# An 8-row tile moved from last to first, and a last 12-row tile summed on two engines and stored in halves

## The chip, the core and the metric

The kernel runs on one core of one Trainium2 chip. The metric is the device time of one execution in microseconds (us); lower is better. Engines that matter: DVE (VectorE), ACT (ScalarE), and the sixteen DMA engines, which move data between the chip's main memory (HBM) and the core's working memory (SBUF, 128 partitions). SP (SyncE) only issues DMAs here.

## What is computed

Each row of 1,024 numbers is divided by the sum of its absolute values.

```python
x = np.random.randn(32, 512, 1024).astype(np.float32)
sums = np.sum(np.abs(x), axis=-1, keepdims=True)
out = (x / (sums + 1e-8)).astype(np.float32)
```

There are 32 x 512 = 16,384 rows of 4 KB: 67.11 MB are read and as many written.

## The kernel before, in words

The 16,384 rows are dealt to 128 partitions, 128 rows each. They are worked through in tiles; `rows` (L31 to L33) is the list of how many rows per partition each tile has: ten tiles of R = 12 and one of the remaining 8, at the end. `piece` (L35) gives tile i's part of the input or output: partition p holds k consecutive rows, so what a DMA moves per partition is one contiguous run (48 KB for 12 rows, 32 KB for 8).

One loop (L70) runs over the tiles, in the order as written. For each tile:

- L72: SP issues one DMA that loads the tile into `x_tile`. The pool `sbuf` has BUFS = 4 buffers, so from the fifth tile on SP waits until the store from four tiles before has landed.
- L45: DVE sums the absolute values of all k rows in one instruction, into `s`. L52 adds EPS and L54 takes the reciprocal, both on k numbers per partition.
- L55: DVE multiplies the first kv = k - k // 3 rows by their reciprocals, in place (8 of 12, 6 of 8). L62: ACT multiplies the other rows, one instruction of 1,024 elements per partition for each (4 of 12, 2 of 8).
- L74: ACT issues one DMA that stores the tile. The issue waits for DVE's multiply and ACT's last row.

Loads thus go through SP's DMA queue (q1 in the profile) and stores through ACT's (q10). Within an engine the order is that of the program; between the engines semaphores order what depends on each other.

Of the kernel before, what the change touches and what calls it, by code (L numbers as in the profile page):

```python
# [1 line left out]

# [4 lines left out]

FP32 = mybir.dt.float32
EPS = 1e-8


@with_exitstack
def kernel(
    ctx: ExitStack,
    tc: tile.TileContext,
    x: bass.AP,
    out: bass.AP,
):
    nc = tc.nc
    P = nc.NUM_PARTITIONS  # L20

    x_flat = x.flatten_outer_dims()
    out_flat = out.flatten_outer_dims()
    n, d = x_flat.shape


    R = 12
    BUFS = 4
    per_partition = n // P
    assert n % P == 0  # L30
    rows = [R] * (per_partition // R)  # L31
    if per_partition % R:
        rows.append(per_partition % R)  # L33

    def piece(flat, i):  # L35
        a, k = P * sum(rows[:i]), rows[i]
        return flat[a : a + P * k, :].rearrange("(p r) d -> p r d", p=P)

    sbuf = ctx.enter_context(tc.tile_pool(name="sbuf", bufs=BUFS))
    stats = ctx.enter_context(tc.tile_pool(name="stats", bufs=4))  # L40

    def normalize(x_tile, r0, k, kv):

        s = stats.tile([P, R], FP32)
        nc.vector.tensor_reduce(  # L45
            out=s[:, :k],
            in_=x_tile[:, r0 : r0 + k, :],
            axis=mybir.AxisListType.X,
            op=mybir.AluOpType.add,
            apply_absolute_value=True,  # L50
        )
        nc.vector.tensor_scalar_add(out=s[:, :k], in0=s[:, :k], scalar1=EPS)  # L52
        inv = stats.tile([P, R], FP32)
        nc.vector.reciprocal(out=inv[:, :k], in_=s[:, :k])  # L54
        nc.vector.tensor_mul(  # L55
            out=x_tile[:, r0 : r0 + kv, :],
            in0=x_tile[:, r0 : r0 + kv, :],
            in1=inv[:, :kv].unsqueeze(2).to_broadcast([P, kv, d]),
        )
        for r in range(kv, k):  # L60
            row = x_tile[:, r0 + r, :]
            nc.scalar.activation(  # L62
                out=row,
                in_=row,
                func=mybir.ActivationFunctionType.Copy,
                scale=inv[:, r : r + 1],
            )

    with tc.manual_schedule():
        for i, k in enumerate(rows):  # L70
            x_tile = sbuf.tile([P, R, d], FP32)
            nc.sync.dma_start(out=x_tile[:, :k, :], in_=piece(x_flat, i))  # L72
            normalize(x_tile, 0, k, k - k // 3)
            nc.scalar.dma_start(out=piece(out_flat, i), in_=x_tile[:, :k, :])  # L74


# [1 line left out]
_INS = ['x']  # L78
_OUTS = [((32, 512, 1024), 'float32')]


# [23 lines left out]
```

## Time and profile before

| | |
|---|---|
| Time, median of 9 executions | 317.2 us (317.08 to 317.56) |
| Time of the profiled execution | 317.41 us |
| Its span in the profile | 315.8 us |
| DVE busy | 235.8 us (75%) |
| ACT busy | 46.1 us (15%) |
| Moved by DMA | 134.23 MB, 425 GB/s over the span |
| Load of a 12-row tile, issue to landing, median | 34.6 us |
| Store of a 12-row tile, issue to landing, median | 51.9 us |

The span runs from the first to the last event that the profiler recorded; the execution's time is 1.6 us longer. In rows of the profile, L45 is line 45 of the kernel, `out<-in` names the buffers, and "idle before" is the time that the engine stood idle just before the instruction, with what ended it. SPq and ACTq are the sequencers of SP and ACT, which issue DMAs; a DMA's own transfer shows in the share of the DMA engines, in the queues' shares, and in the waits of others.

### The profile page before, as it was taken

Reading aid. Unit: us, or ns where it says so; the run is one execution under the profiler, and the core shown is the slowest. Engines: PE = TensorE matmul, PEld = TensorE weight load, DVE = VectorE, ACT = ScalarE, POOL = GpSimd, SP = SyncE. Lnnn points to the kernel's source line nnn. Section 1 sums busy time; section 2 is a strip of 40 time slices with the busy share of each in tenths; the row PEclk is TensorE's granted clock in tenths of the full one; section 3 lists DMA queues with packets and bytes.
Section 4 is the critical chain, followed back from the end, with each engine's and each line's share of the span. In section 5 each row is a group of like instructions: output and inputs, shape, how many; then the busy total and the mean of one; then the engine's idle time right before and its main releaser. Section 6 shows DMA issues by size and latency. Waiting matters only on the chain.

```text
span 315.8 us, 205 instructions
## 1 busy us (share of the span) xinstructions
DVE 235.8 (75%) x44; ACT 46.1 (15%) x43; POOL 0.2 (0%) x4
## 2 busy tenths in 40 slices
DVE  0069999999999599739946991998399569979400
ACT  0010501303105003200500050022005000502000
POOL 0000000000000000000000000000000000000000
DMA  8999999999999999999999999999999999999996
GB/s 324 448 423 423 461 361 442 405 461 436 398 473 423 417 467 411 423 461 411 423 455 417 442 442 411 448 442 411 430 443 417 442 432 446 413 442 448 405 425 299
DMA packets 3169, 134.23 MB, mean 425 GB/s; under 512 B 352, under 2 KB 352, under 8 KB 352
## 3 DMA queue, kind: packets, MB, share of 16 engines
q1 hardware_dynamic: 1584, 67.11, 49.9%
q10 hardware_dynamic: 1584, 67.11, 49.1%
q14 instruction: 1, 0.01, 0.0%
HBM read 67.11 MB, written 67.11 MB: 425 GB/s over the span
## 4 chain that ended last, share of the span: by engine, by line
another core or an unknown queue 36%; DMA 30%; DVE 26%; SPq 0%; issue 0%; DVEq 0%; ACTq 0%
DMA out_dram<-x_tile 15%; DVE s L45 15%; DMA x_tile<-in_x_dram 15%; DVE x_tile L55 10%; SPq L72 0%; DVE inv L54 0%; DVE s L52 0%; DVEq L54 0%; ACTq L74 0%
## 5 line engine op out<-in xcount | busy, mean ns | idle before, releaser
L45 DVE TENSOR_REDUCE s<-x_tile 128x12 f32<-128x12288 f32 (+1 forms) x11 | 138.2, 12563 | 58.0 <-DMA x_tile<-in_x_dram 58.0
L55 DVE TENSOR_TENSOR x_tile<-x_tile,inv 128x8192 f32<-128x8192 f32 (+1 forms) x11 | 93.5, 8498 | 0.4
L62 ACT ACTIVATE x_tile<-x_tile,inv 128x1024 f32<-128x1024 f32 x42 | 44.9, 1136 | 226.5 <-DVE inv L54 226.5
L62 ACT ACT_TABLE_LOAD x1 | 1.3, 1283 | 18.4 <-DMA x_tile<-in_x_dram 18.4
L54 DVE RECIPROCAL inv<-s 128x12 f32<-128x12 f32 (+1 forms) x11 | 2.5, 226 | 0.9
L52 DVE TENSOR_SCALAR s<-s 128x12 f32<-128x12 f32 (+1 forms) x11 | 1.9, 173 | 0.4
L89 POOL MEMSET const-uint8-127<- 128x1 uint8 x1 | 0.1, 102 | 0.0
L89 POOL MEMSET const-bfloat16-1.0<- 128x1 bf16 x1 | 0.1, 101 | 0.0
L89 POOL MEMSET const-float32-0.0<- 128x1 f32 x1 | 0.1, 98 | 0.2 <-issue 0.2
L89 POOL MEMSET const-float32-1.0<- 128x1 f32 x1 | 0.1, 98 | 0.0
## 6 DMA issues: line engine op xcount, KB each, us to landing
x_tile<-in_x_dram SPq DMA_DIRECT2D x10, 6144.0 KB, 34.6
out_dram<-x_tile ACTq DMA_DIRECT2D x10, 6144.0 KB, 51.9
x_tile<-in_x_dram SPq DMA_DIRECT2D x1, 4096.0 KB, 29.5
out_dram<-x_tile ACTq DMA_DIRECT2D x1, 4096.0 KB, 19.2
```

What stands on the lines that cost most here:

```text
L45: nc.vector.tensor_reduce(out=s[:, :k], in_=x_tile[:, r0 : r0 + k, :], axis=mybir.AxisListType.X, op=mybir.AluOpType.add, apply_absolute_v ...
L52: nc.vector.tensor_scalar_add(out=s[:, :k], in0=s[:, :k], scalar1=EPS)
L54: nc.vector.reciprocal(out=inv[:, :k], in_=s[:, :k])
L55: nc.vector.tensor_mul(out=x_tile[:, r0 : r0 + kv, :], in0=x_tile[:, r0 : r0 + kv, :], in1=inv[:, :kv].unsqueeze(2).to_broadcast([P, kv, d]),)
L62: nc.scalar.activation(out=row, in_=row, func=mybir.ActivationFunctionType.Copy, scale=inv[:, r : r + 1],)
L89: nc = _bacc.Bacc("TRN2", target_bir_lowering=False, num_devices=1)
```

## The change

Two things are done together.

The list `rows` gets its 8-row entry in front: the tiles are 8, then ten times 12. The loads of the first four tiles, which wait for no buffer, so cover 44 rows where they covered 48, and the last tile has 12 rows.

The last tile is worked through in two halves of 6 rows, each with a sum, a reciprocal, a multiply and a store of its own. In each half DVE sums 3 rows, and ACT sums the other 3 with one activation (Abs with an accumulator) per row, whose elementwise result goes to a scratch tile `junk` in PSUM, the other on-chip memory. Each of the two engines also multiplies 3 rows. The tile's load stays one DMA. All other tiles are worked as before (`ks` = k; 6 and 2 rows, or 8 and 4, in the multiply).

```diff
     if per_partition % R:
-        rows.append(per_partition % R)
+        rows.insert(0, per_partition % R)
...
+    psum = ctx.enter_context(
+        tc.tile_pool(name="psum", bufs=1, space=bass.MemoryType.PSUM)
+    )
+    junk = psum.tile([P, d], FP32)
+
-    def normalize(x_tile, r0, k, kv):
+    def normalize(x_tile, r0, k, ks, kv):
...
         nc.vector.tensor_reduce(
-            out=s[:, :k],
-            in_=x_tile[:, r0 : r0 + k, :],
+            out=s[:, :ks],
+            in_=x_tile[:, r0 : r0 + ks, :],
...
+        for r in range(ks, k):
+            nc.scalar.activation(
+                out=junk[:, :],
+                in_=x_tile[:, r0 + r, :],
+                func=mybir.ActivationFunctionType.Abs,
+                accum_out=s[:, r : r + 1],
+            )
...
-            normalize(x_tile, 0, k, k - k // 3)
-            nc.scalar.dma_start(out=piece(out_flat, i), in_=x_tile[:, :k, :])
+            final = i == len(rows) - 1
+            h = k // 2 if final else k
+            for r0 in range(0, k, h):
+                if final:
+                    normalize(x_tile, r0, h, h // 2, h // 2)
+                else:
+                    normalize(x_tile, r0, h, h, h - h // 3)
+                nc.scalar.dma_start(
+                    out=piece(out_flat, i)[:, r0 : r0 + h, :],
+                    in_=x_tile[:, r0 : r0 + h, :],
+                )
```

In the built program the order on DVE is, for each half, the sum of 3 rows, the add, the reciprocal and the multiply. On ACT it is three sums, three multiplies and the store's issue for the first half, and then the same for the second; each sum after the first waits for the one before it.

## The prediction

> **What bounds the kernel now.** I read the page first: the share of the DMA queues, before any engine.
>
> ```profile
> span 315.8 us, 205 instructions
> ...
> DVE 235.8 (75%) x44; ACT 46.1 (15%) x43; POOL 0.2 (0%) x4
> ...
> DMA  8999999999999999999999999999999999999996
> ...
> q1 hardware_dynamic: 1584, 67.11, 49.9%
> q10 hardware_dynamic: 1584, 67.11, 49.1%
> ```
>
> The two queues, q1 for loads (issued by SP) and q10 for stores (issued by ACT), fill 49.9 + 49.1 = 99.0% of the sixteen DMA engines' time: 312.6 us of 315.8. No order of the work can win more than the 3.2 us left, unless the packets themselves become shorter. Next, where those 3.2 us lie: busy time by stretches (columns: stretch, its length, DVE, ACT, POOL busy, clock, DMA share, GB/s).
>
> ```profile
> 0.00:2.00 2.00, 0.00 (x0) 0.00 (x0) 0.20 (x4) 1.00 1.01 295
> 2.00:250.00 248.00, 198.14 (x36) 39.68 (x37) 0.00 (x0) 1.00 1.00 429
> 250.00:279.65 29.65, 22.05 (x4) 4.26 (x4) 0.00 (x0) 1.00 1.00 433
> 279.65:295.54 15.89, 15.62 (x4) 2.19 (x2) 0.00 (x0) 1.00 1.01 439
> 295.54:313.40 17.86, 0.00 (x0) 0.00 (x0) 0.00 (x0) 1.00 0.96 416
> 313.40:315.80 2.40, 0.00 (x0) 0.00 (x0) 0.00 (x0) 1.00 0.00 0
> ```
>
> The share is 1.00 from 2 us to the last store's issue at 295.54. A packet is counted where it starts, so the last two rows say: packets go out until the end of the drain, and then the last ones finish. By the trace's packet records the first starts at 1.72 us and the last ends at 314.35; a packet of 49,152 B (one partition of a 12-row tile) takes 1.815 us in the median, one of 32,768 B 1.213 us. Each engine carries 8 packets of each tile: 20 x 8 x 1.815 + 2 x 8 x 1.213 = 309.8 us. The rest up to 312.5 us is slow packets: 0.8 us per engine at the first load, 1.15 us around 42 us, shortly after the first store is issued (40.62), some 0.5 us between 148 and 231.
>
> Third, the end, in order of time, where a summary of the chain would name the vector engine:
>
> ```profile
> 277.79 0.34 ACTq L74 DMA_DIRECT2D out_dram<-x_tile  x1
> 279.65 8.69 DVE L45 TENSOR_REDUCE s<-x_tile 128x8 f32<-128x8192 f32 x1 [1.96 <-DMA x_tile<-in_x_dram]
> 288.38 0.17 DVE L52 TENSOR_SCALAR s<-s 128x8 f32<-128x8 f32 x1
> 288.65 0.20 DVE L54 RECIPROCAL inv<-s 128x8 f32<-128x8 f32 x1
> 288.89 6.56 DVE L55 TENSOR_TENSOR x_tile<-x_tile,inv 128x6144 f32<-128x6144 f32 x1
> 288.89 2.19 ACT L62 ACTIVATE x_tile<-x_tile,inv 128x1024 f32<-128x1024 f32 x2 [15.62 <-DVE inv L54]
> 295.54 0.34 ACTq L74 DMA_DIRECT2D out_dram<-x_tile  x1
> ```
>
> The last tile takes 15.89 us from landing to the store's issue, and it looks like the tail. It isn't: at 439 GB/s the engines are meanwhile draining earlier stores, and the packet records put the last packet of the store before it at 304.67, 9.1 us after the last store is queued.
>
> **What the Trainium skill says.** "DMA: Bandwidth & Descriptors", section "Queues, rings and completion order": each DMA engine takes turns between the queues that have work, packet by packet. The trace agrees: a 12-row load alone takes 8 x 1.815 = 14.5 us, beside stores 29.0 us (tiles land at 226.46 and 255.48). Its section "Where 436 GB/s comes from" puts the ceiling at 435 GB/s and says that HBM traffic is held to about 358; the trace has 429 to 439, so the ceiling holds here and the lower figure doesn't. "ScalarE: Activation LUTs", section "What ACT_TABLE_LOAD costs", prices an activation at 186 ns + 0.833 ns per element, and 93 ns for a per-partition operand: 1.132 us for L62, as traced (1.132 in the median); its section "Table sets: the hidden batching unit" says that abs is in every set, so Abs beside Copy needs no second table load.
>
> **The change part by part.**
>
> Durations, from the groups by form (busy, mean ns):
>
> ```profile
> L45 DVE TENSOR_REDUCE s<-x_tile 128x12 f32<-128x12288 f32 x10 | 129.5, 12951 | 56.1 <-DMA x_tile<-in_x_dram 56.1
> L55 DVE TENSOR_TENSOR x_tile<-x_tile,inv 128x8192 f32<-128x8192 f32 x10 | 86.9, 8692 | 0.3
> ```
>
> With the 8-row forms above, a row costs (12.95 - 8.69) / 4 = 1.066 us in the sum, with 0.16 fixed, and the same in the multiply ((8.69 - 6.56) / 2).
>
> *Packets.* The bytes stay. The last tile's store becomes two, so each engine gets 16 packets of 24,576 B for 8 of 49,152. From the two sizes a packet costs 11 ns + 0.0367 ns per byte, so 8 x 11 = 0.09 us more, and one more completion packet of 9 ns: +0.1 us. Lower bound 0; upper bound 0.3 us, if the fixed part were thrice as large on shorter packets.
>
> *The 8-row tile first.* It lands 14.5 - 9.7 = 4.8 us sooner, at 18.39 - 4.8 = 13.6, and is stored after 15.9 us, at 29.5 instead of 40.62. This starts stores 11 us earlier and gains nothing, since until then the loads fill the engines. Four loads are still in flight, 44 rows for 48. First packet of store 0: 4.4 us after its issue, as before (45.04 against 40.62), so 33.9. Then 8 turns of 1.213 + 1.815: done at 58.1, landed at 60.3 (2.2 us after the last packet, as for the loads: 253.29 and 255.48). SP's wait for it (the fifth load's) is covered: of the 24 load packets after tile 0, 11 are through at 33.9 and 8 more at 58.1; 5 are left, 18 us in turns. Store 1 is issued at 29.5 + 22.1 = 51.6, before store 0 ends.
>
> *The end.* Now both queues take turns, 8 x 3.63 = 29.04 us per 12-row tile. Store k ends at 58.1 + 29.04k, load 3 at 58.1 + 5 x 3.63 = 76.3, load 10 at 76.3 + 7 x 29.04 = 279.6; it lands at 281.8. Tile 9 lands at 252.7 and its store is queued at 274.9. Store 7 ends at 261.4; store 8 takes 5 turns beside loads until 279.6, then 3 packets alone: 285.0. Store 9: 285.0 + 14.5 = 299.5. So the engines have other work until 299.5, and half 1 has to be queued by then, less a lead of up to 4.4 us as at the first store.
>
> *The halves.* Half 1: DVE sums 3 rows in 3 x 1.066 + 0.16 = 3.4 us, beside it ACT sums 3. The trace has no Abs with an accumulator. Lower bound: the skill's 1.04 us each, 3.1 us. Upper bound: 1.13 us plus 0.4 for the accumulator and the wait on ACT's own semaphore that the build puts between them, 4.6. I take 3.6. The add and the reciprocal with gaps: 0.6. Multiply: DVE 3 rows, 3.4, beside three ACT rows at 1.07 each. Issue 0.1: 7.7 us in all (7.5 to 8.7), at 289.5. Half 2: DVE goes straight on; ACT's three sums are queued behind the store's issue, which waits for DVE's multiply: 0.4 more, 8.1 us, so 297.6 (to 299.5). Half 1's packets keep the engines until 299.5 + 7.3 = 306.8. Both are queued 9 to 10 us ahead (7 at the upper bounds), so summing on both engines and the split cost and bring nothing in time; DVE was idle before this tile lands (274.9 to 281.8), so nothing waits behind them.
>
> What if that cover were absent? A plain 12-row tile takes 22.1 us from landing to store: 281.8 + 22.3 = 304.1, that is 4.6 us after the engines run out, plus a lead of up to 4.4. So moving the 8-row tile alone costs 4.6 to 9 us, and the halves take exactly that back. Sum against the profiled execution (317.41 us, span 315.8): +0.1, 317.5. It lies 0.2 over the median of 317.2, so against the median: 317.3.
>
> **The rivals.** *Faster: the slow packets go.* The 1.15 us at the first store could fall away or be shared with the cold first loads, as the store now comes earlier; or the engines' ends, spread over 313.17 to 314.35, draw together with half-sized packets. For it: nothing else in the span is loose. Against it: the loads in flight at the first store are as many as before. 317.3 - 1.15 = 316.1.
>
> *Slower: the store queue starts cold twice.* Store 1 is queued 6.5 us before store 0 ends; with the lead of 4.4 us only 2.1 us are left. If store 0 is quicker by over 2.1 us, the queue runs dry near 56 us and may stall the loads by 1.15 us again: 318.4. Against it: the engines go on loading, and the stall may belong to the very first use.
>
> *Slower: the tail is bare.* If ACT's sums are far dearer, half 1 misses 299.5. It decides from 17.7 us (less the lead, 13.3) between landing and store. At the plain tile's 22.3 us: 317.3 + 4.6 = 321.9 or more. Against it: it needs sums of over 3 us a row where the price is 1.1.
>
> **How the numbers follow.** Forecast (no change; its own range 316.8 to 317.9): 0.78. Slow packets gone: 0.10. Cold start twice: 0.07. Bare tail: 0.05. About 0.2% (0.63 us) is what a measurement of this kernel can tell from no change, so faster 0.10, same 0.78, slower 0.12. The range goes from 316.4, most of the way to the faster case, to 318.4, the cold start; the bare tail and the rest of the faster case stay outside.
>
> **What would show it.** The two queues again at 99% of the engines; the last load landing near 282; two stores issued near 290 and 298 while the DMA share stays at 1.00 until about 313; one table load; the first store issued near 29.5. I'm wrong if the DMA share drops before the drain (near 56 us or after 299), or if the slow load packets at the first store are missing or come twice.

## The result, and the profile after

The changed kernel takes 319.52 us (median of 9 executions, 319.19 to 320.07) against 317.24 (29 executions): a ratio of 1.007, 95% interval 1.0062 to 1.0079. That is 2.3 us slower, outside the predicted range of 316.4 to 318.4. Its profiled execution took 319.41 us, with a span of 317.6. Three more executions took 319.91, 317.49 and 322.76 us; they are not among the nine, and the last counts as a slow run.

The page of the changed kernel, the lines that answer to those of before:

```profile
span 317.6 us, 226 instructions
...
DVE 228.0 (72%) x48; ACT 55.2 (17%) x57; POOL 0.2 (0%) x4
...
DMA  8999999999999999999999999999999999999994
...
q1 hardware_dynamic: 1584, 67.11, 49.5%
q10 hardware_dynamic: 1728, 67.11, 48.8%
```

The queues' share fell from 99.0% to 98.3%, but of a longer span: 0.983 x 317.6 = 312.2 us, as good as the 312.6 before. So the packets cost what they did. What was added is time in which DMA engines do nothing, and the stretches say where (columns as in the prediction):

```profile
2.00:284.10 282.10, 213.94 (x40) 41.87 (x39) 0.00 (x0) 1.00 1.00 430
284.10:299.35 15.25, 14.06 (x8) 13.34 (x18) 0.00 (x0) 1.00 0.97 418
299.35:312.00 12.65, 0.00 (x0) 0.00 (x0) 0.00 (x0) 1.00 1.00 431
312.00:313.00 1.00, 0.00 (x0) 0.00 (x0) 0.00 (x0) 1.00 0.97 418
313.00:314.00 1.00, 0.00 (x0) 0.00 (x0) 0.00 (x0) 1.00 0.23 98
314.00:315.00 1.00, 0.00 (x0) 0.00 (x0) 0.00 (x0) 1.00 0.17 74
315.00:316.00 1.00, 0.00 (x0) 0.00 (x0) 0.00 (x0) 1.00 0.06 25
```

There is no hole in the middle and none before the drain. The end is ragged instead. One packet of 24,576 B started in a stretch of 1 us shows as 25 GB/s: from 315 to 316 us, one of sixteen engines starts one packet, and the other fifteen have none left to start. The kernel before, in the same stretches, starts no data packet after 314 us:

```profile
312.00:313.00 1.00, 0.00 (x0) 0.00 (x0) 0.00 (x0) 1.00 0.91 393
313.00:314.00 1.00, 0.00 (x0) 0.00 (x0) 0.00 (x0) 1.00 0.23 98
314.00:315.00 1.00, 0.00 (x0) 0.00 (x0) 0.00 (x0) 1.00 0.00 0
```

The packet records show the same engine by engine. (Packets carry no engine number; I followed each engine from one packet's end to the next one's start. The completion packets of the last store, 4 B each and one per engine, give the same ends without that.)

| us | before | after |
|---|---|---|
| Mean of the sixteen engines' last packets | 313.82 | 313.84 |
| First engine done | 313.17 | 313.03 |
| Last engine done | 314.35 | 316.43 |
| Time of the profiled execution less the last engine's end | 3.06 | 2.98 |

The mean moved by 0.02 us; the last engine moved by 2.08, and the time with it. A slow packet is one that takes longer than the median of its size (1.815 us for 49,152 B); what counts below is the excess. After 60 us, three engines of the changed kernel collect 1.42, 1.60 and 2.43 us of it, while nine have 0.1 us or less. Before, each engine had between 0.3 and 0.9.

The end on the compute engines is as planned:

```profile
284.12 3.35 DVE L52 TENSOR_REDUCE s<-x_tile 128x3 f32<-128x3072 f32 x1 [6.98 <-DMA x_tile<-in_x_dram]
285.08 0.19 ACT L60 ACTIVATION_READ_ACCUMULATOR junk<-x_tile 128x1 f32 x1
285.30 1.03 ACT L60 ACTIVATE junk<-x_tile 128x1024 f32<-128x1024 f32 x1
...
287.66 0.17 DVE L66 TENSOR_SCALAR s<-s 128x6 f32<-128x6 f32 x1 [0.19 <-ACT junk L60]
...
291.54 0.34 ACTq L96 DMA_DIRECT2D out_dram<-x_tile  x1
...
299.35 0.34 ACTq L96 DMA_DIRECT2D out_dram<-x_tile  x1
```

The first half takes 7.4 us from landing to store, the second 7.8. The tile lands at 284.12 where I had 281.8: a load has landed when its last engine is done, so the landing waits for the straggler too. In a trace of the same kernel without stragglers (number 5 below) the tile landed at 281.38.

### The profile page after: what moved, and what is told of

Read it like the earlier page. It is cut to its first block, busy times and chain, and to the rows that moved or that the text cites. A ratio compares the mean times of both kernels' runs of the same rounds, so it can differ in the third digit from the quotient of the medians.

```text
span 317.6 us, 226 instructions
## 1 busy us (share of the span) xinstructions
DVE 228.0 (72%) x48; ACT 55.2 (17%) x57; POOL 0.2 (0%) x4
## 4 chain that ended last, share of the span: by engine, by line
DVE 49%; DMA 31%; another core or an unknown queue 11%; ACT 2%; issue 1%; ACTq 0%; DVEq 0%; SPq 0%
DVE s L52 27%; DVE x_tile L69 21%; DMA x_tile<-in_x_dram 19%; DMA out_dram<-x_tile 11%; ACT junk L60 2%; DVE inv L68 1%; DVE s L66 1%; ACTq L96 0%; DVEq L68 0%; SPq L86 0%
## 5 line engine op out<-in xcount | busy, mean ns | idle before, releaser
L52 DVE TENSOR_REDUCE s<-x_tile 128x12 f32<-128x12288 f32 (+2 forms) x12 | 132.0, 10996 | 68.7 <-DMA x_tile<-in_x_dram 68.7
L69 DVE TENSOR_TENSOR x_tile<-x_tile,inv 128x8192 f32<-128x8192 f32 (+2 forms) x12 | 91.5, 7625 | 0.4
L76 ACT ACTIVATE x_tile<-x_tile,inv 128x1024 f32<-128x1024 f32 x44 | 47.0, 1137 | 218.8 <-DVE inv L68 218.8
L60 ACT ACTIVATE junk<-x_tile 128x1024 f32<-128x1024 f32 x6 | 6.2, 1028 | 12.1 <-DMA x_tile<-in_x_dram 11.4
L68 DVE RECIPROCAL inv<-s 128x12 f32<-128x12 f32 (+2 forms) x12 | 2.6, 220 | 0.8
L66 DVE TENSOR_SCALAR s<-s 128x12 f32<-128x12 f32 (+2 forms) x12 | 2.1, 173 | 1.3 <-ACT junk L60 0.9
L60 ACT ACTIVATION_READ_ACCUMULATOR junk<-x_tile 128x1 f32 x6 | 1.1, 186 | 0.0
```

The costliest lines, as they stand in the source:

```text
L52: nc.vector.tensor_reduce(out=s[:, :ks], in_=x_tile[:, r0 : r0 + ks, :], axis=mybir.AxisListType.X, op=mybir.AluOpType.add, apply_absolute ...
L60: nc.scalar.activation(out=junk[:, :], in_=x_tile[:, r0 + r, :], func=mybir.ActivationFunctionType.Abs, accum_out=s[:, r : r + 1],)
L69: nc.vector.tensor_mul(out=x_tile[:, r0 : r0 + kv, :], in0=x_tile[:, r0 : r0 + kv, :], in1=inv[:, :kv].unsqueeze(2).to_broadcast([P, kv, d]),)
L76: nc.scalar.activation(out=row, in_=row, func=mybir.ActivationFunctionType.Copy, scale=inv[:, r : r + 1],)
```

## The experiments

Each was timed beside the kernel before on the same chip. "Order" below names the tile order, "stragglers" the engines that end late, with more than 1.3 us of slow packets after 60 us. The time of the profiled execution is the last engine's end plus 2.92 to 3.09 us in every trace below.

**1. The order alone.** The last 12-row tile is worked like every other.

```diff
-            final = i == len(rows) - 1
+            final = False
```

> The 8-row tile first, the last 12-row tile as every other: one sum on DVE, one store. Theory 'stragglers' (the order makes slow load packets pile up on a few of the sixteen DMA engines; the halves cost nothing): three engines again collect 1.4 to 2.4 us of slow packets after 60 us, as in the changed kernel, and in addition the tail is bare, so the DMA share drops to near 0 before the last store's packets: the last store issued near 306.4 (284.1 + 22.3), first packet up to 4.4 us later, time 324 to 328 us. Theory 'halves' (the two smaller stores and ACT's sums cost the 2.3 us): no straggling engines; the bare tail alone, 322 to 326 us, with the engines' ends within 1.3 us of each other.

Measured: 325.0 us (322.0 to 325.8; ratio 1.022, interval 1.019 to 1.026). The stretches of its end:

```profile
284.30:300.00 15.70, 15.46 (x4) 2.10 (x3) 0.00 (x0) 1.00 0.82 354
300.00:303.00 3.00, 3.00 (x1) 2.16 (x3) 0.00 (x0) 1.00 0.04 16
303.00:307.50 4.50, 3.59 (x1) 0.00 (x0) 0.00 (x0) 1.00 0.00 0
307.50:322.00 14.50, 0.00 (x0) 0.00 (x0) 0.00 (x0) 1.00 1.01 434
```

The engines run dry near 300 us, stand still until the last store's packets start at 307.5, and then need 14.5 us for it. The tail is bare as worked out: 7.8 us slower than before, inside the 4.6 to 9 of the prediction. All engines end within 0.15 us here, as they start the last store together, so this run says nothing on what stragglers cost; its trace has one engine with 2.8 us of slow packets after 60 us, where the theory 'stragglers' forecast three.

**2. The halves alone.** The 8-row tile stays last and is worked in halves of 4.

```diff
-        rows.insert(0, per_partition % R)
+        rows.append(per_partition % R)
```

> The 8-row tile stays last and is worked in halves of 4 rows, summed on both engines, with two stores. Theory 'stragglers': same as the kernel before, 317.2 us (317.0 to 317.6), the engines' last packets end within 1.3 us of each other. Theory 'halves': 319 to 319.8 us, with the spread of the ends appearing only in the last 40 us.

Measured: 317.38 us, ratio 1.0003 (0.9991 to 1.0015). Halves of the 8-row tile, smaller packets and ACT's sums cost nothing that shows.

**3 and 4. The moment of the first store.** DVE multiplies one row more of the first tile, so that its store comes later; in the changed kernel and in the one before.

```diff
-                    normalize(x_tile, r0, h, h, h - h // 3)
+                    normalize(x_tile, r0, h, h, h - h // 3 + (i == 0))
```

```diff
-            normalize(x_tile, 0, k, k - k // 3)
+            normalize(x_tile, 0, k, k - k // 3 + (i == 0))
```

> The changed kernel, but DVE multiplies 7 of the first tile's 8 rows in place of 6, so that the first store and all DVE work after it come 1.07 us later (0.59 of a 1.815 us load packet). Theory 'moment' (which engines straggle is set by where in the load packets the first store comes in, the order matters only through that): the straggling changes, time 317.0 to 318.5 us. Theory 'order' (the order itself brings it, whatever the moment): 319.2 to 320.1 us as in the changed kernel.

> The kernel before, but DVE multiplies 9 of the first tile's 12 rows in place of 8, so that its first store comes 1.07 us later. Theory 'moment': the time moves by over 0.3 us, to 318 or more if engines straggle here as well, with the mean end of the engines unchanged near 313.7. Theory 'order': 317.2 us as before (317.0 to 317.6).

Measured: the changed kernel with this edit takes 317.12 us (ratio 1.0002, 0.9983 to 1.0021), one of 14 executions above 318.5. The kernel before with it takes 317.89 (1.0023, 1.0006 to 1.0040), with four of 21 above 318.5. One row's multiply on another engine, hidden behind the DMA in both, moves the two kernels in opposite directions.

**5. The changed kernel again.** No edit.

> The changed kernel itself, unedited, once more beside the variants of its first tile. If the 2.3 us belong to the kernel: 319.2 to 320.1 us again, with three or four engines collecting over 1.3 us of slow packets each and the others next to none. If they belonged to the chip or the hour of the first measurement: 317.0 to 318.0 us, and then the variant with 7 rows on DVE showed nothing.

Measured: 319.4 us; five executions lie at 319.1 to 320.1 and one at 317.21, and that one was profiled. Its end:

```profile
312.00:313.00 1.00, 0.00 (x0) 0.00 (x0) 0.00 (x0) 1.00 0.91 393
313.00:314.00 1.00, 0.00 (x0) 0.00 (x0) 0.00 (x0) 1.00 0.07 25
314.00:315.00 1.00, 0.00 (x0) 0.00 (x0) 0.00 (x0) 1.00 0.00 0
```

The last engine ends at 314.12, and no engine has over 0.36 us of slow packets after 60 us. The same program, with the stragglers and without: 319.41 and 317.21 us. This pair is the closest to a measurement of what they cost, though it isn't clean: the engines' mean end differs too, by 0.38 us (313.84 and 313.46).

**6 and 7. Other moments.** The same edit as in 3 with `- (i == 0)` (5 rows, store 1.07 us earlier) and `+ 2 * (i == 0)` (8 rows, 2.13 us later).

> The changed kernel, DVE multiplies 5 of the first tile's 8 rows, so that its store and DVE's next sum come 1.07 us earlier. Theory 'moment': another place in the 1.815 us load packets (0.41 of a packet on, counted round), so the time leaves 319.5, to 316.8 to 318.5 us. Theory 'order': 319.2 to 320.1 us.

> The changed kernel, DVE multiplies all 8 rows of the first tile, so that its store comes 2.13 us later, 1.17 packets. Theory 'moment': nearly the same place in a packet as the changed kernel (0.17 on), so it should straggle again, 318.5 to 320 us. Theory 'later is better' (anything that comes later than in the changed kernel avoids the clash): 317.0 to 317.6 us. Theory 'order': 319.2 to 320.1 us.

Measured: 5 rows 317.04 us (0.9996, 0.9987 to 1.0006). 8 rows 317.31, in two heaps: 16 of 22 executions at 316.6 to 318.1, six at 319.5 to 321.2. So neither "later is better" nor "order" holds. "Moment" got the direction with 5 rows, but had forecast that 8 rows would straggle again, and 16 of the 22 executions show no sign of it.

**8. The 8-row tile second.** `rows.insert(1, ...)`, halves at the end.

> The 8-row tile comes second in place of first; the last 12-row tile in halves on both engines. The first tile and the first store are as in the kernel before (store issued near 40.6 us). Theory 'moment': as the kernel before, 317.0 to 317.8 us, since the first store meets the loads in the same place. Theory 'order' (an 8-row tile ahead of the 12-row ones makes the straggling): 319 to 320 us.

Measured: 318.85 us (1.0066, 1.0035 to 1.0096). This went against "moment of the first store": that store is issued at 40.29, near the 40.62 of before, and all sixteen engines still collect 0.7 to 2.6 us of slow packets after 60 us. The second store comes at 55.92 instead of 62.68. The test isn't exact, as the first store is 0.33 us earlier, but the first store can hardly be the only moment that counts.

**9. An attempt that missed.** ACT copies a row to `junk` ahead of the first store's issue.

```diff
+                if i == 0:
+                    nc.scalar.activation(
+                        out=junk[:, :],
+                        in_=x_tile[:, 0, :],
+                        func=mybir.ActivationFunctionType.Copy,
+                    )
```

> The changed kernel, but ACT copies one row that DVE has just multiplied into the scratch tile before it issues the first store: the store comes 1.0 to 1.1 us later, while DVE's order and times stay. Theory 'moment of the first store': most runs leave 319.5 and lie at 316.6 to 317.6 us, as with 7 rows on DVE (317.12). Theory 'DVE' (the later variants were faster since all DVE work moved, not since the first store did): 319.1 to 320.1 us in most runs.

Measured: 318.49 us (317.33 to 320.37). The edit did not do what it was for: the store doesn't depend on the copy, and both started at 29.11 us, 0.39 us later than in the changed kernel's trace, as the first load landed 0.44 us later. It is inconclusive on the moment. But the profiled execution, 320.37 us, shows a straggler at its plainest:

```profile
312.00:313.00 1.00, 0.00 (x0) 0.00 (x0) 0.00 (x0) 1.00 0.35 148
313.00:314.00 1.00, 0.00 (x0) 0.00 (x0) 0.00 (x0) 1.00 0.06 25
314.00:315.00 1.00, 0.00 (x0) 0.00 (x0) 0.00 (x0) 1.00 0.06 25
315.00:316.00 1.00, 0.00 (x0) 0.00 (x0) 0.00 (x0) 1.00 0.06 25
316.00:317.00 1.00, 0.00 (x0) 0.00 (x0) 0.00 (x0) 1.00 0.06 25
```

One packet in each microsecond: fifteen engines end by 313.42, the sixteenth at 317.39.

**10 and 11. An early DMA on ACT's queue**, in the kernel before and in the 5-row variant.

```diff
     with tc.manual_schedule():
+        warm = stats.tile([P, R], FP32)
+        nc.scalar.dma_start(out=warm[:, :1], in_=x_flat[:P, :1])
```

> The kernel before, with one small DMA added on ACT's queue at the very start (128 partitions of 4 B, read into a scratch tile that nothing uses). Theory 'cold queue' (the slow load packets near 42 us, 1.1 us per engine, come from the first use of ACT's queue): they vanish or move to the start, and the time falls by up to 1.1 us, to 316.1 to 316.9. Theory 'meeting' (they come from stores joining loads in flight): they stay, 317.0 to 317.7 us.

> The changed kernel with 5 of the first tile's 8 rows on DVE (317.04 us) and the same small early DMA on ACT's queue. Theory 'cold queue': the 0.8 us per engine at the first store go, 316.0 to 316.5 us. Theory 'meeting': 316.6 to 317.6 us. If the early DMA moves the loads' place in time as well, the engines may straggle again, 319 us or more in some runs.

Measured: before with it 318.20 us (1.0027, 1.0010 to 1.0044), the 5-row variant 316.82 (0.9978, 0.9969 to 0.9986). "Cold queue" falls: the slow packets at the first store stay, 1.02 us per engine near 42 us in the first, 0.93 near 30 us in the second. The forecast of 316.6 to 317.6 for the second came in. That for the first did not, under either theory: ten of its 22 executions lie above 318.5 us, against three of 41 of the kernel before on the same chip. Why the early DMA slows this kernel stays open; the profiled execution is not one of the ten (317.56 us).

**12. The first store later, DVE untouched.** As in 9, but the copy goes onto the row itself (its values stay), so the store has to wait.

```diff
+                        out=x_tile[:, 0, :],
+                        in_=x_tile[:, 0, :],
```

> The changed kernel, but ACT copies one row that DVE has multiplied onto itself before it issues the first store; since the store reads that row, it now has to wait: it comes 1.1 us later, while DVE's order and times stay. Theory 'moment of the first store': nearly no straggling, 316.6 to 317.7 us in most runs, as with 7 rows on DVE. Theory 'DVE' (it was the moved DVE work that helped): 319.1 to 320.1 us in most runs, beside the unedited kernel of the same call.

Measured: 316.90 us (0.9995, 0.9982 to 1.0007); 21 of 22 executions at 316.5 to 317.5. The unedited kernel took 319.45 us on the same chip (number 15 below). The delay, in order of time; the unedited kernel issues this store at 28.72:

```profile
28.69 12.94 DVE L52 TENSOR_REDUCE s<-x_tile 128x12 f32<-128x12288 f32 x1
28.80 1.06 ACT L97 ACTIVATE x_tile<-x_tile 128x1024 f32<-128x1024 f32 x1 [4.40 <-DVE x_tile L69]
29.89 0.37 ACTq L102 DMA_DIRECT2D out_dram<-x_tile  x1
```

DVE's sum starts at 28.69 against 28.55, and only the store moved, by 1.17 us. A copy that changes no value takes 2.5 us off the time.

**13 to 15. On one chip: 5 rows again, all stores in two DMAs, the unedited kernel.** In number 14 each tile's store is issued as two DMAs of half its rows (the last tile's halves stay one each):

```diff
+                for q in (r0,) if final else (r0, r0 + h // 2):
+                    nc.scalar.dma_start(
+                        out=piece(out_flat, i)[:, q : q + (h if final else h // 2), :],
+                        in_=x_tile[:, q : q + (h if final else h // 2), :],
+                    )
```

> The changed kernel with 5 of the first tile's 8 rows on DVE, again, on whatever chip this call gets. If its 317.04 us belong to the kernel: 316.6 to 317.6 us in nearly all runs and below the kernel before, 0.1% to 0.2%. If they belonged to that chip: straggling runs at 319 us or more among them.

> The changed kernel with every store, not the last tile's alone, issued as two DMAs of half the rows: twice the completion packets beside the loads. Theory 'completion' (the slow load packets are those right behind a store's completion packet on the same engine): about twice as many places to be slow, so 2 to 5 us of slow packets on the worst engine and 319 us or more, or, if the halves change the turns, at least more engines with slow packets after 60 us than in the unedited kernel, each behind a completion. Theory 'address' (they come from where data lies): slow packets as many as in the unedited kernel, 319.2 to 320.1 us.

> The changed kernel unedited, on the same chip as the three above. Most runs at 319 to 320.1 us, one in six or so near 317.3, and the slower ones with one to three engines that end over 1.5 us after the others.

Measured: 5 rows 317.92 us (1.0016, 1.0000 to 1.0031), three of 14 executions over 318.5; on the chip of number 6 none of 14 were. So the executions above 318.5 us of that variant come and go, and the forecast of 316.6 to 317.6 in nearly all runs failed here. Stores in two: 318.24 (1.0045, 1.0022 to 1.0069). Its slow packets aren't doubled: they reach all sixteen engines in one spell from 60 to 83 us, some right behind a completion packet and some not, and after that few are left. "Completion" is not borne out, and the time that either theory forecast, 319 us or more, did not come in. The unedited kernel: 319.45, four of six executions above 319.4, the others at 317.73 (the profiled one) and 318.09.

**16 to 18. Which variants hold.** 7 rows again, 5 rows with the early DMA again, and 7 rows with the early DMA.

> The changed kernel with 7 of the first tile's 8 rows on DVE, again, on whatever chip this call gets. Theory 'moment of the first store': 316.6 to 317.6 us in nine runs of ten, no slower than the kernel before. If the 317.12 us belonged to that chip: a third of the runs or more over 318.5 us.

> The changed kernel with 5 rows of the first tile on DVE and a small early DMA on ACT's queue, again. If its 316.82 us (0.2% below the kernel before) belong to the kernel: 316.5 to 317.2 us. If to the chip, as with 5 rows alone (317.04 us on one chip, 317.92 on another): 317.5 us or more, with straggling engines in some runs.

> The changed kernel with 7 rows of the first tile on DVE and the small early DMA on ACT's queue. Theory 'moment of the first store': the first store's moment is that of the 7-row variant but for about 0.1 us, so 316.6 to 317.6 us; the early DMA by itself brings nothing, since the slow packets at the first store stayed when it was tried before.

Measured: 317.31 us (1.0003, 0.9987 to 1.0020), 316.77 (0.9978, 0.9965 to 0.9990), 317.03 (0.9992, 0.9984 to 1.0000). Number 17 repeats number 11 on another chip: the changed kernel with 5 rows of its first tile on DVE and the early DMA beats both kernels: by 0.2% the one before, and by some 0.9% the changed one (0.9978 / 1.007). All its 37 executions lie under 317.5. Its end in number 17:

```profile
311.00:312.00 1.00, 0.00 (x0) 0.00 (x0) 0.00 (x0) 1.00 1.08 467
312.00:313.00 1.00, 0.00 (x0) 0.00 (x0) 0.00 (x0) 1.00 0.52 221
313.00:314.00 1.00, 0.00 (x0) 0.00 (x0) 0.00 (x0) 1.00 0.00 0
```

The mean end is 313.06 and the last 313.83. What the early DMA adds wasn't measured against 5 rows alone on one chip.

The count of timed executions above 318.5 us: the changed kernel 18 of 21; 8 rows 6 of 22; 5 rows 3 of 28; 7 rows 2 of 27; first store later 1 of 22; 7 rows with the early DMA none of 13; 5 rows with the early DMA none of 37; the kernel before, timed beside the experiments, 9 of 211.

## Why the prediction was wrong

*The bound.* Right: DMA engines are the limit in both kernels, and their mean end, 313.82 and 313.84, did not move. One reading was loose: 439 GB/s lies above the 435 of the ceiling that the prediction says holds. Packets are counted where they start, and over the long stretch of 248 us the figure is 429.

*The packets.* Right: 24,576 B take 0.912 us, so two cost 0.01 us more than one of 49,152, 0.1 us per engine in all.

*The 8-row tile first.* Right in its times: landed at 12.91 (13.6 predicted), first store issued at 28.72 (29.5), its first packet at 32.84 (33.9), the fifth load covered.

*The end and the halves.* Right: both stores were queued before the engines needed them (the first at 291.54 us, its first packet at 298.48), one sum on ACT takes 1.03 us and 0.19 to read the accumulator (1.2 taken), and no second table load appears. Taken alone, the order costs 7.8 us (number 1), inside the 4.6 to 9 worked out, and halves nothing (number 2, with halves of 4 rows).

*The slow packets: here it failed.* I wrote that "the rest up to 312.5 us is slow packets" per engine, a mean over sixteen, and carried it over unchanged. The time is set by the slowest engine, not by the mean. The mean of all slow packets is 2.47 us before and 2.40 after, but the engine that ends last has 2.43 us of them after 60 us, where the one that ended last before had 0.38: 2.05 of the 2.1 us. What came earlier nearly cancels (1.66 us at the first load and 1.06 at the first store before; 0.06 and 1.73 after, on an engine that began its first packet 0.9 us later). Before, a second engine ended within 0.01 us of the last; it had 0.57 us after 60 us, which gives the same picture. I did look at the spread of the ends, but only as something that could draw together ("slow packets go"), never as something that could grow. That was the missing rival.

*The rivals.* The slow packets at the first store neither went nor came twice: 1.33 us per engine once (1.15 before), and none near 56 us. The tail wasn't bare.

*What sets it, as far as the runs show.* In the kernel as changed, the first store's moment makes the difference: number 12 moves that alone, by 1.17 us, and 21 of 22 executions stay below 318.5 us, against two of six of the unedited kernel on the same chip.

The packet records show what the moment changes: how many load packets each engine has started before its first store packet.

| Trace | Load packets before the first store packet | First store packets start at, us |
|---|---|---|
| Changed kernel | 19 on six engines, 20 on ten | 32.84 to 33.22; 35.04 to 35.29 |
| Number 5, unedited, no straggler | 19 on eight, 20 on eight | 32.97 to 33.36; 35.16 to 35.63 |
| Number 6, 5 rows | 19 on all sixteen | 32.90 to 33.36 |
| Number 12, first store later | 20 on all sixteen | 34.58 to 35.12 |
| Number 7, 8 rows | 21 on all sixteen | 36.51 to 37.09 |

So in the changed kernel the first store catches some engines before the start of a load packet and others after it, and from then on they take turns out of step: the fifth load's sixteen completion packets come in two groups, ten at 104.53 to 104.78 us and six at 107.04 to 107.32, in number 12 in one, 104.07 to 104.60. The traces of all variants with another moment (3, 6, 7, 11 to 13, 16 to 18) have one group at the first store. They also have less slow time there, 0.7 to 0.9 us per engine against 1.3 in the three traces of the unedited kernel, and an earlier mean end, 313.0 to 313.2 us against 313.5 to 313.8. So part of what a moved store gains lies with all engines, and the rest with the stragglers. All these variants were profiled in an execution below 317.5 us, so their rare executions above 318.5 us aren't seen.

The three stragglers are among the six early engines. Number 9's trace has one early engine, with its first store packet at 33.31 us where the fifteen others have theirs at 34.62 to 34.94, and that one is the straggler. The engine with 2.8 us of slow packets in number 1 is again the only early one, 33.05 against 34.54 or later.

Two groups alone don't make stragglers: number 5, number 15 (19 load packets on ten engines, 20 on six) and the kernel before (ten engines at 45.04 to 46.28 us, six at 47.23 to 47.91) have two groups and none. Nor is one group at the first store enough to avoid slow packets: number 8 has one, 45.15 to 46.06, and they reach all sixteen engines. In the changed kernel's trace most of the large slow packets after 60 us are loads right behind a store's completion packet on the same engine, but number 14, made to multiply those, did not multiply them. Why a load packet becomes slow, and why it keeps hitting the same engine, stays open; so does why the 8-row tile in second place (number 8) slows all sixteen.

## What to carry to other kernels

Where DMA engines are full from start to end, as here, a mean share of 99% doesn't give the time; the last of the sixteen engines does. Look at the last microseconds in narrow stretches: 25 GB/s there was one engine working while fifteen were done. Here a hidden edit early on, worth nothing by the sum, moved the time by 0.8% down (number 12) or 0.2% up (number 4), so give the spread of the engines' ends its own place in the range, on both sides, and try a shift of the first store by a microsecond before judging the rest of a change.

## What the runs showed that I had not expected

- The same program ends at 317.2 or at 319.4 us, with the engines' mean end 0.4 us apart (313.46 and 313.84) and the last engine's 2.3 us (314.12 and 316.43).
- One microsecond in the issue of a store decides whether the sixteen engines meet it after the same number of load packets, and engines that parted there were still parted 70 us later.
- One engine alone can fall 4 us behind the other fifteen (number 9), and nothing later brings it back: by the packet records each of the sixteen carries 207 packets, whether late or not.
- An activation with an accumulator is two instructions on ACT: 1.03 us for 1,024 elements into PSUM, and 0.19 us for the read of the accumulator.
